# Two-layer diffusion backbone: one turn for the context units' weights, the keys' rotation summed on VectorE, and new planning constants

## The chip, the cores and the metric

The kernel runs on one core of a Trainium2 chip. The metric is the device time of one execution in microseconds (us). The core has five engines that are named here as the profile names them: PE (TensorE, the matmuls), DVE (VectorE), ACT (ScalarE), POOL (GpSimd) and SP (SyncE, which here issues DMAs). PEld is the loading of stationary operands into PE. A `q` behind an engine (SPq, ACTq) marks what its sequencer does, such as issuing a DMA.

## The reference

512 latent tokens and 256 context tokens, all of width 1024, go through two layers. Both layers share this frame:

```python
h = rms_norm(x, pre_g[i]) * (1.0 + scale) + shift
hc = rms_norm(xc, pre_g[i]) * (1.0 + cscale) + cshift
...
x = x + gate * rms_norm(y, post_g[i])
if not last:
    xc = xc + cgate * rms_norm(yc, post_g[i])
```

`shift`, `scale` and `gate` come from a product of a conditioning vector with `ada_w`. The mixer of layer 0 is differential attention with 8 heads of two 64-wide halves, that of layer 1 is attention with 8 query heads of width 128, two key and value heads, and normalised queries and keys. Both rotate the queries and keys of the latent tokens. Context queries see context keys alone, latent queries see all 768 keys. The result of a head is multiplied by `silu(z)`, and `w_out` maps the branch back to 1024 columns.

```python
o1 = sweep_attention(qq[..., 0, :], kk[..., 0, :], vv)
o2 = sweep_attention(qq[..., 1, :], kk[..., 1, :], vv)
o = o1 - lam.astype(o1.dtype) * o2
o = rms_norm(o, subln_g) * (1.0 - lam_init)
return (o.reshape(o.shape[0], o.shape[1], BRANCH_WIDTH) * jax.nn.silu(gate)) @ w_out
```

```python
def apply_rope(x, cos, sin):
    x1, x2 = jnp.split(x, 2, axis=-1)
    return jnp.concatenate([x1 * cs - x2 * sn, x2 * cs + x1 * sn], axis=-1)
```

In layer 1 only the latent tokens have queries, since the context's result is not used.

## The kernel before

**Precision.** Each projection multiplies a high and a low half of both operands: `mm3` (L174 and on) issues three matmuls, high by high, high by low, low by high, through `tmm` (L166 to L172, so L170 stands for most matmuls of the trace). A weight is loaded by SP into `raw`, cast to its high half on ACT (L249, `whi`), and the rest is taken by `pieces` (L240 to L243, `wlo`) on DVE, or on POOL in pieces of 256 columns.

**Layer 0, attention.** `s_units` makes one unit per 128 queries: scores on PE (L1055 for a latent unit, L1087 for a context one), maximum on DVE (L1060), exponential on ACT (L1063), the difference of the two softmaxes on DVE, then `f_split` makes two float16 halves of the weights: `fp` by ACT (L291) and DVE (L1025). `f_turn` (L1030) turns them so that keys stand on the partitions: a transposing DMA from SP (`turn`, L253 and L254) writes them into `ft`. A tile `ft` of 12 rows of 256 serves two units, the even one's 128 queries in the left half of each row and the odd one's in the right. `unit_ctx` (L1080 and on) does both context units of a head together, for heads 0 to 6: their weights are two times 512 columns, and two DMAs turn them, one for each block of 128 queries. Head 7's context goes through two plain units. `pv_f16` (L184 to L187) multiplies the values with the turned weights, six matmuls of 256 columns for two rows of keys: 18 for a chunk of two latent units, 6 for the context chunk.

**Layer boundary.** Layer 0's output projection and residual end in `h1_tr` (L1401 and on): PE transposes the normalised rows (L1406), DVE and ACT scale and shift four tiles of 256 columns into `hf` (the first HFD of each four on DVE, L1412, the rest on ACT, L1414), ACT casts the high half (L1418) and DVE takes the low half (L1419). The list KV orders the keys' and values' projection: `k` a projection, `t` an `h1_tr`, `c` the transposes of one finished block of keys (`k_tr`, L1473 and on). A block of keys is normalised (`head_rstd`, L1459 to L1466; L1487), rotated by `rope_tok` (products ta, L1452, and tb, L1454, on DVE; their sum on POOL, L1457, written to `kr`), and transposed on PE (L1477). KVE tells on which engine the low halves of weights 8 to 11 are taken (1 is POOL). `rope_tok` also serves the queries of layer 1.

**Layer 1, attention.** `s1_units` makes a unit per 128 queries and head (maximum L1590, exponential L1596, float16 halves L291 and L1602), turned by one full DMA each; `pv1_steps` uses two of them per chunk. `q_proj` and `z1_proj` are the projections that fill the time between. At the end `tail1` splits the results (L1681, L1682) and starts the last output projection on the banks of the scores.

**What sets the order.** The program text is emitted by a planner, `flow`. It keeps a clock of PE time. Each `Step` (a score unit, a use of turned weights, a loading of conditioning weights) has a due time `at` and lags behind other steps; while no step is due, `piece()` emits one matmul triple of the filling work (projections in the order of FILL0 or FILL1). In layer 0 a head's share of the clock is `per = ATT + DL0[h] + filling`, where `filling` is 7.7 us for a `z` and 15.4 us for a `qk` or a `v` that HF0 lists for that head; its six units are due at even distances over `per - GAP0 + jt[5]`, jt being the row of JT for that layer and head. `acc_steps` spreads the conditioning weights' steps over the heads by ACCN. In layer 1 a unit is due at

```python
st_.at = at_ + TS * (h * 2 + ch + i / 2) + jt[0][5]
```

where `at_` is AT1 after the first queries' projection. A use of turned weights is due LA + jt[0] after its last unit and LT + jt[1] after the use before it; a score unit waits SLAG (SLAG1 in layer 1) + jt[4] behind an earlier one; LM and jt[2] are lags of a step for the output; HOT0, HOT1 and jt[3] are priorities. The framework then arranges the instructions of each engine by these priorities. Tile names that occur below: `sc` scores in PSUM, `p` exponentials, `vp` values, `gT` and `g1` (shown as `g`) results, `araw` and `gw` conditioning weights, `xn` normalised rows.

Of the kernel before, what the change touches and what calls it, by code (L numbers as in the profile page):

```python
# [12 lines left out]
ALU = mybir.AluOpType  # L13
# [6 lines left out]
P = 128  # L20
# [9 lines left out]
SC_A = 64 ** -0.5  # L30
SC_B = 128 ** -0.5
HOT = 1357
HF0 = ((('z', 0), ('qk', 1), ('qk', 2), ('qk', 3)), (), (('z', 1), ('qk', 4), ('v', 2), ('z', 2)), (), (('qk', 5), ('z', 3), ('v', 4), ('qk', 6), ('z', 4)), (), (('qk', 7), ('z', 6), ('v', 6), ('z', 5), ('z', 7)), ())
FILL0 = tuple(f for hf in HF0 for f in hf)
ATT = 15.11
ACCN = (1, 0, 4, 2, 4, 0, 3, 4)
ACD = 1.77
FILL1 = (('q', 1), ('z', 2), ('z', 0), ('q', 2), ('q', 3), ('z', 1), ('z', 3), ('z', 4), ('z', 6), ('z', 5), ('z', 7))
HOT0 = (3826, 1502, 326, 3469)
HOT1 = (2169, 4095, 3201, 5846, 2552, 918)  # L40
WARM = 3008
AGB = 10
PRE = 19.12
TS = 8.25
HFD = 2
KVE = (1, 0, 0, 0)
KV = (('k', 0), ('t', 1), ('k', 2), ('k', 1), ('t', 0), ('c', 1), ('k', 3), ('c', 0), ('k', 4), ('c', 2), ('c', 3), ('k', 5))
SPL = 7.5
GAP0 = 5.92
DL0 = (4.7, -1.53, 0.38, 0.81, 1.04, 3.67, -0.34, 6.0)  # L50
WBUFS = 3
XE = [2, 2, 2, 2, 3, 3]
NWARM = 16
# [18 lines left out]
HFB = 3  # L72
PRI = (3010, 72, 362, 216, 1000)
GD = (2.08, 2.79)
QLAG = 3.92
QTR = 9.95
EG0 = 'a'
EP0 = 'p'
# [2 lines left out]
EG1 = 'a'  # L81
EGA = "v"
RL = 4.05
LM = (4.63, 10.94)
PB0 = 3
FB0 = 2
EF0 = 'a'
VH = 2.6
VPB = 1
FT0 = 3  # L90
JT = (((-1.05, -0.92, 0.68, 2264, 0.12, 3.56), (0, 0.85, 1.39, -990, 0.72, 0.2), (-2.31, -0.09, 3.54, 1893, 0.76, -2.98), (-0.99, -0.17, -1.19, 0, 0.9, 0.95), (0.7, 0.62, -0.38, -4, 2.54, -1.23), (-0.72, 0.43, 0.01, -269, -0.45, -2.95), (1.4, 0.1, 0.12, -328, 0.12, -0.89), (0.18, -0.06, 1.09, 0, -2.44, -0.17)), ((-3.15, 0.21, -0.44, -128, 2.28, 0.69), (1.27, -0.8, -0.1, 65, -0.08, 1.07), (-2.3, -0.84, -1.14, 69, -0.88, 0), (1.25, 0.04, 0, 721, -0.58, -0.62), (0.58, -0.04, 0.52, 604, 0.04, 0.06), (0.41, -0.95, -2.95, 60, -1.31, -1.14), (0.75, -0.49, -1.4, 1427, 0, -1.44), (0.04, 0.48, -1.17, 217, 1.04, 0.15)))


def f32(ap):
# [8 lines left out]
def tile_backbone(  # L103
# [23 lines left out]
    nc = tc.nc  # L127
# [125 lines left out]
    def turn(dst, src):  # L253
        nc.sync.dma_start(dst, src, transpose=True)  # L254
# [604 lines left out]
    with tc.tile_pool(name="t0", bufs=1) as t0:  # L859
# [32 lines left out]
        qk, pend, qk_t = {}, {}, {}  # L892
# [134 lines left out]
        def ft_tile():  # L1027
            return t0.tile([P, 12, 256], F16, tag="ft", name=nm("ft"), bufs=FT0)

        def f_turn(ft, fp, e):  # L1030
            turn(ft[:, :4 * fp.shape[1], e * P:e * P + P], fp.rearrange("p j a n -> p (j a n)"))

        def s_units(h, qts):
            res = []
# [42 lines left out]
            def unit_ctx():  # L1077
                sc = [sc2(), sc2()]
                qh, ql, kh_, kl_ = qk[h]
                prev = None  # L1080
                for qt in (NQ, NQ + 1):
                    tok = slice(qt * P, (qt + 1) * P)
                    for i, (a, b) in enumerate(((qh, kh_), (qh, kl_), (ql, kh_))):
                        for m in (1, 0):
                            r = slice(m * 64, m * 64 + 64)
                            with onward(prev):
                                prev = nc.tensor.matmul(  # L1087
                                    sc[m][:, qt - NQ, :C], a[r, tok], b[r, S:T], start=i == 0, stop=i == 2)
                l = small(4)
                pts = []  # L1090
                for m in range(2):
                    mx = small(2)
                    nc.vector.tensor_reduce(mx, sc[m][:, :, :C], AX.X, ALU.max, negate=True)
                    pt = t0.tile([P, T], F32, tag=f"p{m}", name=nm("p"), bufs=PB0 if m == 0 else 2)
                    pts.append([pt[:, e * C:(e + 1) * C] for e in range(2)])
                    for e in range(2):
                        nc.scalar.activation(pts[m][e], sc[m][:, e, :C], AF.Exp, bias=mx[:, e:e + 1], accum_out=l[:, 2 * m + e:2 * m + e + 1])
                r, f = small(4), small(4)
                nc.vector.reciprocal(r, l)
                nc.vector.scalar_tensor_tensor(f[:, 0:2], r[:, 2:4], nlam, l[:, 0:2], ALU.mult, ALU.mult)  # L1100
                nc.vector.tensor_scalar(f[:, 2:4], r[:, 0:2], psc[:, 0:1], None, ALU.mult)
                fp = f_tile()
                for e in range(2):
                    nc.vector.scalar_tensor_tensor(pts[0][e], pts[1][e], f[:, e:e + 1], pts[0][e], ALU.mult, ALU.add)  # L1104
                    f_split(fp[:, e], pts[0][e], f[:, 2 + e:3 + e])
                res.append(ft_tile())
                for e in range(2):
                    f_turn(res[0], fp[:, e:e + 1], e)

            if qts[0] == NQ and h < KT - 1:  # L1110
                return res, [Step(unit_ctx, 1.0)]
# [244 lines left out]
    c, n = OUTC[0]  # L1356
# [13 lines left out]
    c, n = OUTC[1]  # L1370
# [63 lines left out]
    with tc.tile_pool(name="t1", bufs=1, side="right") as t1p:  # L1434
# [9 lines left out]
        kl = t1p.tile([P, 2, T], F32R, name="kl")  # L1444
        vp = t1p.tile([P, 2, NT, 256], F16, name="vp")

        def rope_tok(dst, src, t):
            n = 2
            s3 = src.rearrange("p (h d) -> p h d", h=n)
            ta_ = t1p.tile([P, n, P], F32, tag="ta", name=nm("ta"), bufs=2)  # L1450
            tb_ = t1p.tile([P, n, P], F32, tag="tb", name=nm("tb"), bufs=1)
            nc.vector.tensor_tensor(ta_, s3, cosb[:, t, :].unsqueeze(1).to_broadcast([P, n, P]), ALU.mult)  # L1452
            for j in range(2):
                nc.vector.tensor_tensor(  # L1454
                    tb_[:, :, j * 64:j * 64 + 64], s3[:, :, (1 - j) * 64:(1 - j) * 64 + 64],
                    sinb[:, t, j * 64:j * 64 + 64].unsqueeze(1).to_broadcast([P, n, 64]), ALU.mult)
            nc.gpsimd.tensor_tensor(dst.rearrange("p (h d) -> p h d", h=n), ta_, tb_, ALU.add)  # L1457
# [25 lines left out]
        def k_rope(m, o, r):  # L1483
            kn = t1p.tile([P, 256], F32, tag="qt", name=nm("kn"), bufs=9)
            for j in range(2):
                sl = slice(j * P, (j + 1) * P)
                nc.vector.scalar_tensor_tensor(kn[:, sl], o[:, sl], r[:, j:j + 1], gq[:, 1, :], ALU.mult, ALU.mult)  # L1487
            close(o)
            if m < NQ:
                kr = t1p.tile([P, 256], F32, tag="qt", name=nm("kr"), bufs=9)  # L1490
                rope_tok(kr, kn, m)
            else:
                kr = kn
            ktr.append((m, kr))
# [260 lines left out]
        c, n = OUTC1[0]  # L1755
# [9 lines left out]
        c, n = OUTC1[1]  # L1765
# [134 lines left out]
```

## Time and profile before

| what | value |
|---|---|
| time, median of 3 runs | 742.33 us |
| lowest and highest of them | 741.08 and 743.64 us |
| profiled execution, its own time | 742.18 us |
| its span, first to last instruction | 740.1 us |
| granted TensorE clock, mean | 0.997 |
| HBM read, written | 70.56 MB, 2.10 MB |

In the profile, busy times are of instructions that do work; issuing a DMA and waiting are not counted. Matmuls are pipelined and their ends are modelled, so the mean duration of one is longer than the distance between two. A row of the timeline gives the start, the duration of the merged instructions, the engine, the line, the operation, output and inputs with their shapes, and the count; in brackets stands the engine's idle time just before it and what ended it. A row of waits gives, for an engine and line, what it waited for, the sum, the number of times and the longest.

### The profile page before, as it was taken

The numbers are of one execution on the slowest core, as the hardware profiler recorded it, in microseconds if no ns is written. First come the engines' busy times: TensorE is split into PE (matmuls) and PEld (weight loads), VectorE is DVE, ScalarE is ACT, GpSimd is POOL, SyncE is SP. The second block draws the span as 40 slices with busy tenths as digits, with TensorE's granted clock in tenths as the row PEclk, the third lists the DMA queues.
The fourth block names the chain that finished last, engine by engine and source line by source line (L and its number), as shares of the span: only waits on it lengthen the run. The fifth ranks groups of instructions, "written<-read, shape, count | busy, mean of one in ns | idle before, by whom it ended". The sixth has DMA issues, their size and how long they took to land. (4 is left out here: it accounts for less than half of the span.)

```text
span 740.1 us, 12749 instructions
## 1 busy us (share of the span) xinstructions
PE 722.6 (98%) x4668; PEld 615.9 (83%) x4668; DVE 523.0 (71%) x947; ACT 484.0 (65%) x1016; POOL 247.4 (33%) x334
## 2 busy tenths in 40 slices
PE   8999999999999999999999999998999999999996
PEld 6789888878987888889878888877998999887785
DVE  4667566789777777777777815387668889877724
ACT  5547456686676685777877734485548777788622
POOL 0110236553412633445131411554452534143101
PEclk9999999999999999999999999999999999999998
DMA  9935363455757434754565207030436798887503
GB/s 332 391 112 196 110 171 94 113 133 147 173 134 192 107 92 113 195 108 138 134 153 146 58 8 255 30 115 19 141 105 138 150 207 183 207 177 130 123 26 113
DMA packets 142093, 104.93 MB, mean 142 GB/s; under 512 B 112464, under 2 KB 115024, under 8 KB 142032
## 3 DMA queue, kind: packets, MB, share of 16 engines
q1 hardware_dynamic: 138176, 98.32, 51.5%
q10 hardware_dynamic: 3856, 5.81, 2.3%
q8 instruction: 36, 0.59, 0.3%
q14 instruction: 25, 0.20, 0.1%
HBM read 70.56 MB, written 2.10 MB: 98 GB/s over the span
## 5 line engine op out<-in xcount | busy, mean ns | idle before, releaser
L170 PE MATMUL bk<-h,whi 128*128 128x512 f32 (+2 forms) x864 | 228.1, 347 | 0.1
L170 PE MATMUL bk<-whi,h 128*128 128x256 f32 (+1 forms) x928 | 214.6, 319 | 0.0
L170 PEld LDWEIGHTS bk<-whi,h 128*128 128x128 f32 x928 | 155.2, 189 | 16.5 <-issue 3.7
L170 PEld LDWEIGHTS bk<-h,whi 128*128 128x128 f32 x864 | 151.0, 188 | 19.2 <-issue 2.7
L170 PE MATMUL bk<-h,wlo 128*128 128x512 f32 (+2 forms) x432 | 149.0, 346 | 0.0
L170 PE MATMUL bk<-wlo,h 128*128 128x256 f32 (+1 forms) x464 | 146.3, 317 | 0.0
L243 DVE TENSOR_TENSOR wlo<-raw,whi 128x1024 fp32r<-128x1024 f32 (+2 forms) x70 | 83.6, 1197 | 21.9 <-ACT whi L249 21.3
L170 PEld LDWEIGHTS bk<-wlo,h 128*128 128x128 f32 x464 | 87.5, 189 | 5.9
L170 PEld LDWEIGHTS bk<-h,wlo 128*128 128x128 f32 x432 | 81.1, 188 | 8.6 <-issue 1.6
L291 ACT ACTIVATE fp<-p,sm 128x768 f16<-128x768 f32 (+1 forms) x80 | 67.6, 851 | 28.6 <-DVE p L1104 9.5
L243 POOL TENSOR_TENSOR sz<-sz,za 128x192 f32<-128x192 f32 (+1 forms) x48 | 34.8, 748 | 151.0 <-ACT za L223 151.0
L187 PE MATMUL bk<-ft,vp 128*128 128x256 f16 x624 | 78.7, 274 | 4.7 <-DMA ft<-fp 4.5
L249 ACT CAST whi<-raw 128x1024 fp32r<-128x1024 f32 x64 | 67.0, 1047 | 22.2 <-PE bk L170 10.1
L187 PEld LDWEIGHTS <-vp 128*128 128x128 f16 x624 | 57.2, 98 | 23.5 <-issue 9.4
L1063 ACT ACTIVATE p<-sc,sm 128x768 f32<-128x768 f32 (+1 forms) x68 | 59.5, 877 | 21.6 <-DVE sm L1060 20.5
L1060 DVE TENSOR_REDUCE sm<-sc 128x1 f32<-128x768 f32 (+1 forms) x68 | 60.6, 918 | 9.6 <-PE sc L1055 9.4
L1025 DVE SCALAR_TENSOR_TENSOR fp<-p,sm,fp 128x768 f16<-128x768 f32 (+1 forms) x48 | 43.8, 922 | 14.1 <-ACT fp L291 13.8
L1055 PE MATMUL sc<-qk,qk 64*128 64x384 f32 (+1 forms) x396 | 43.6, 351 | 0.5 <-ACT p L1063 0.3
L243 POOL TENSOR_TENSOR qk<-qr,qk 128x256 fp32r<-128x256 f32 x42 | 31.7, 790 | 36.2 <-ACT qk L932 36.2
L170 PE MATMUL sc<-whi,h 128*128 128x512 f32 x128 | 41.9, 395 | 1.0 <-ACT p L1596 1.0
L1055 PEld LDWEIGHTS sc<-qk,qk 64*128 64x128 f32 x396 | 32.8, 184 | 8.3 <-issue 4.1
L243 POOL TENSOR_TENSOR qr<-qr,sw 128x256 f32<-128x256 f32 x28 | 24.3, 888 | 39.3 <-DVE sw L917 39.3
(254 smaller groups left out, 1207.7 us busy)
## 6 DMA issues: line engine op xcount, KB each, us to landing
raw<-in_a_w SPq DMA_DIRECT2D x28, 512.0 KB, 3.4
araw<-in_ada_w SPq DMA_DIRECT2D x12, 1024.0 KB, 5.5
raw<-in_b_w SPq DMA_DIRECT2D x20, 512.0 KB, 3.4
ag<-in_ada SPq DMA_DIRECT2D x16, 512.0 KB, 7.9
raw<-in_w_out SPq DMA_DIRECT2D x16, 512.0 KB, 4.6
sw<-qr ACTq DMA_DIRECT2D x32, 128.0 KB, 2.1
gw<-in_ada_w SPq DMA_DIRECT2D x8, 512.0 KB, 4.1
xnt<-in_xlT SPq DMA_DIRECT2D x4, 512.0 KB, 5.9
```

The costliest lines, as they stand in the source:

```text
L170: i = nc.tensor.matmul(o, a, b, start=start, stop=stop)
L187: nc.tensor.matmul(o, v[:, a, kt + e, c], f[:, 2 * b + e, :], start=first and i == 0, stop=last and i == 5)
L243: eng.tensor_tensor(dst[:, i:i + n], a[:, i:i + n], b[:, i:i + n], op)
L249: nc.scalar.copy(hi, r)
L291: nc.scalar.activation(dst, src, AF.Copy, scale=s_)
L1025: nc.vector.scalar_tensor_tensor(fp[..., 1, :], src, r, fp[..., 0, :], ALU.mult, ALU.subtract)
L1055: prev = nc.tensor.matmul(sc[m][:, j if nk == T else m, :w], a[r, tok], b[r, c], start=i == 0, stop=i == 2)
L1060: nc.vector.tensor_reduce(mx, scv, AX.XY if nk == T else AX.X, ALU.max, negate=True)
L1063: nc.scalar.activation(pv_, scv, AF.Exp, bias=mx, accum_out=l[:, m:m + 1])
```

## The change

Four edits of the code, and new values of constants.

- `unit_ctx` turns the weights of both context units with one DMA into the first 1024 columns of the tile's row, block of 128 queries by block. A small class, `CtxF`, gives `pv_f16` the same view as before: for each key row, two runs of 128 columns.
- `rope_tok` has a new argument: the sum of ta and tb is on DVE when it is set. `k_rope` sets it, the queries do not.
- KVE goes from (1, 0, 0, 0) to zeros: the low half of weight 8 is taken on DVE. HFD goes from 2 to 3: of four scalings in `h1_tr` three are on DVE.
- The planner's constants change for both layers. In HF0, `z` 6 is now ahead of `qk` 7, and `z` 7 is counted to head 7 instead of head 6.

```diff
-HF0 = (..., (), (('qk', 7), ('z', 6), ('v', 6), ('z', 5), ('z', 7)), ())
+HF0 = (..., (), (('z', 6), ('qk', 7), ('v', 6), ('z', 5)), (('z', 7),))
-ACCN = (1, 0, 4, 2, 4, 0, 3, 4)
+ACCN = (1, 0, 4, 4, 1, 1, 3, 4)
-HOT1 = (2169, 4095, 3201, 5846, 2552, 918)
+HOT1 = (2621, 4095, 3201, 5846, 2552, 801)
-TS = 8.25
-HFD = 2
-KVE = (1, 0, 0, 0)
+TS = 8.28
+HFD = 3
+KVE = (0, 0, 0, 0)
-DL0 = (4.7, -1.53, 0.38, 0.81, 1.04, 3.67, -0.34, 6.0)
+DL0 = (4.7, -1.53, 2.15, 0.81, 1.04, 3.37, -0.34, 6.0)
-LA = (12.0, 7.03)
-LT = (1.27, 1.11)
+LA = (12.0, 6.91)
+LT = (1.27, 0.75)
-SLAG1 = 2.79
-AT1 = 7.65
+SLAG1 = 1.91
+AT1 = 6.52
-QLAG = 3.92
+QLAG = 4.06
-LM = (4.63, 10.94)
+LM = (4.63, 10.89)
-JT = (((-1.05, -0.92, 0.68, 2264, 0.12, 3.56), (0, 0.85, 1.39, -990, 0.72, 0.2), (-2.31, -0.09, 3.54, 1893, 0.76, -2.98), (-0.99, -0.17, -1.19, 0, 0.9, 0.95), (0.7, 0.62, -0.38, -4, 2.54, -1.23), (-0.72, 0.43, 0.01, -269, -0.45, -2.95), (1.4, 0.1, 0.12, -328, 0.12, -0.89), (0.18, -0.06, 1.09, 0, -2.44, -0.17)), ((-3.15, 0.21, -0.44, -128, 2.28, 0.69), (1.27, -0.8, -0.1, 65, -0.08, 1.07), (-2.3, -0.84, -1.14, 69, -0.88, 0), (1.25, 0.04, 0, 721, -0.58, -0.62), (0.58, -0.04, 0.52, 604, 0.04, 0.06), (0.41, -0.95, -2.95, 60, -1.31, -1.14), (0.75, -0.49, -1.4, 1427, 0, -1.44), (0.04, 0.48, -1.17, 217, 1.04, 0.15)))
+JT = (((-1.05, -0.92, 0.68, 2264, 0.12, 3.56), (0, 0.85, 1.39, -990, 0.72, 0.2), (-1.79, -0.04, 3.05, 2086, 0.25, -3.11), (-1.27, -0.19, -1.34, -101, 0.52, 1.62), (0.7, 0.62, -0.38, 172, 2.54, -1.23), (-2.89, 0.39, 0.58, -269, -0.21, -5.24), (1.4, 0.1, 0.12, -328, 0.12, -0.89), (0.18, -0.06, 1.09, 0, -2.44, -0.17)), ((-3.15, 0.14, -0.44, 0, 1.76, 0.45), (1.27, -0.86, -1.1, 65, 0.0, 1.07), (-2.3, -0.67, -1.14, -156, -1.53, 0), (1.25, 0.05, 0.3, -218, -0.19, -0.62), (3.23, 0.88, 1.15, 604, -2.1, 0), (0.41, -0.95, -4.08, 60, -1.31, -0.92), (0, -0.65, -0.83, 1758, 0, -2.55), (-0.45, 0.78, -0.94, -466, 1.04, 0.14)))
...
+        class CtxF:
+            def __init__(self, ft):
+                self.f = ft.rearrange("p j n -> p (j n)")[:, :1024].rearrange("p (e j n) -> p j e n", e=2, n=P)
+
+            def __getitem__(self, i):
+                return self.f if i[1] == slice(0, 4) else self.f[:, i[1]]
...
-                res.append(ft_tile())
-                for e in range(2):
-                    f_turn(res[0], fp[:, e:e + 1], e)
+                ft = ft_tile()
+                turn(ft.rearrange("p j (b n) -> p (j b) n", n=P)[:, :8], fp[:, :2].rearrange("p e a n -> p (e a n)"))
+                res.append(CtxF(ft))
...
-            nc.gpsimd.tensor_tensor(dst.rearrange("p (h d) -> p h d", h=n), ta_, tb_, ALU.add)
+            (nc.vector if ev else nc.gpsimd).tensor_tensor(dst.rearrange("p (h d) -> p h d", h=n), ta_, tb_, ALU.add)
...
-                rope_tok(kr, kn, m)
+                rope_tok(kr, kn, m, True)
```

More of the change, by code (lines that the diff above doesn't have):

```diff
@@ L32 @@
 HOT = 1357
-HF0 = ((('z', 0), ('qk', 1), ('qk', 2), ('qk', 3)), (), (('z', 1), ('qk', 4), ('v', 2), ('z', 2)), (), (('qk', 5), ('z', 3), ('v', 4), ('qk', 6), ('z', 4)), (), (('qk', 7), ('z', 6), ('v', 6), ('z', 5), ('z', 7)), ())
+HF0 = ((('z', 0), ('qk', 1), ('qk', 2), ('qk', 3)), (), (('z', 1), ('qk', 4), ('v', 2), ('z', 2)), (), (('qk', 5), ('z', 3), ('v', 4), ('qk', 6), ('z', 4)), (), (('z', 6), ('qk', 7), ('v', 6), ('z', 5)), (('z', 7),))
 FILL0 = tuple(f for hf in HF0 for f in hf)
 ATT = 15.11
-ACCN = (1, 0, 4, 2, 4, 0, 3, 4)
+ACCN = (1, 0, 4, 4, 1, 1, 3, 4)
 ACD = 1.77
@@ L1445, in tile_backbone, with rope_tok @@
         vp = t1p.tile([P, 2, NT, 256], F16, name="vp")
-        def rope_tok(dst, src, t):
+        def rope_tok(dst, src, t, ev=False):
             n = 2
```

## Prediction

> **What bounds the kernel now.** I read the page first, then PE's waits by releaser, then the stages, and last the timeline around each wait. The first lines are the page's, the next are those of PE's waits (total us, times, longest), the last are rows of the stage table (length, PE, PEld, DVE, ACT and POOL busy).
>
> ```profile
> span 740.1 us, 12749 instructions
> ```
>
> ```profile
> PE 722.6 (98%) x4668; PEld 615.9 (83%) x4668; DVE 523.0 (71%) x947; ACT 484.0 (65%) x1016; POOL 247.4 (33%) x334
> ```
>
> ```profile
> PE bk L187 <- DMA ft<-fp: 4.5, 4, 1.8
> PE bk L1477 <- POOL kr L1457: 1.9, 1, 1.9
> PE sc L170 <- ACT p L1596: 1.0, 1, 1.0
> ```
>
> ```profile
> 0.00:45.00 45.00, 41.95 (x306) 31.69 (x307) 28.38 (x83) 24.66 (x50) 4.56 (x11) 1.00 0.90 331
> 234.00:265.00 31.00, 29.41 (x210) 26.18 (x209) 23.85 (x38) 21.71 (x49) 13.58 (x16) 1.00 0.49 112
> 370.00:410.00 40.00, 38.23 (x283) 31.83 (x283) 30.29 (x53) 29.66 (x63) 11.84 (x16) 1.00 0.56 139
> 470.00:532.00 62.00, 59.84 (x315) 49.47 (x314) 43.60 (x85) 38.73 (x111) 30.77 (x52) 1.00 0.23 71
> 532.00:600.00 68.00, 67.86 (x495) 64.66 (x495) 52.66 (x117) 47.52 (x110) 28.19 (x42) 1.00 0.61 141
> 660.00:690.00 30.00, 27.27 (x155) 22.95 (x154) 24.41 (x42) 25.67 (x44) 10.81 (x12) 1.00 0.66 124
> 690.00:741.00 51.00, 44.00 (x213) 35.91 (x211) 22.84 (x35) 15.86 (x34) 4.72 (x12) 0.95 0.33 94
> ```
>
> TensorE is the bound: 722.6 of 740.1 us. No matmul is added or removed, so the change can only act through the 17.5 us in which PE is idle. Of these the first 45 us hold 3.05 and the last stage 6.1 (51.00 less 0.9 beyond the span, less 44.00); both run code that the diff leaves alone. What is left to win is 1.59 + 1.77 + 2.16 + 0.14 + 2.73 = 8.4 us, five stages with a handful of waits. What can be lost has no such limit: PE works through its queue in the order that is set, so any producer that is late by an order set anew stops it.
>
> **The change part by part.**
>
> *The keys' sum on VectorE.* The longest single wait of the layer boundary, row by row (start, duration, engine, line, what it waited for in brackets), and below it the groups that price the sum on either engine:
>
> ```profile
> 512.87 0.42 DVE L1452 TENSOR_TENSOR ta<-kn,ropeb 128x256 f32<-128x256 f32 x1
> 513.21 0.49 DVE L1454 TENSOR_TENSOR tb<-kn,ropeb 128x128 f32<-128x128 f32 x2
> 513.62 0.68 DVE L1419 TENSOR_TENSOR h<-hf,h 128x512 fp32r<-128x512 f32 x1
> 513.78 1.10 POOL L1457 TENSOR_TENSOR kr<-ta,tb 128x256 f32<-128x256 f32 x1 [1.59 <-DVE tb L1454]
> 514.94 0.44 PE L1477 MATMUL bk<-ident,kr 128*128 128x128 f32 x2 [1.94 <-POOL kr L1457]
> ```
>
> ```profile
> L1457 POOL TENSOR_TENSOR kr<-ta,tb 128x256 f32<-128x256 f32 x4 | 3.3, 830 | 5.6 <-DVE tb L1454 5.6
> L1481 DVE TENSOR_TENSOR kl<-bk,kh 128x256 fp32r<-128x256 f32 x5 | 2.1, 414 | 0.0
> ```
>
> On POOL the sum ran 513.78 to 514.88. On VectorE a sum of this shape takes 0.41 us and can follow tb at 513.70: it ends at 514.11 if nothing is put between, 0.77 us sooner, and at 514.8 if one 0.68 us pass of h goes first, 0.1 sooner. The order in the queues is planned too, and a sum that is known to end sooner may have its transposes put elsewhere; then all 1.94 goes. So the gain is 0.1 to 1.94, and I take 1.2, between the row's 0.77 and the whole wait. The four sums add 4 x 0.41 = 1.7 us to VectorE, which is 43.60 us busy of 62 here. Behind each stand the h passes of the boundary, for which the next projection waits.
>
> In the rows above, the POOL sum that starts within the h pass of VectorE took 1.10 us, where its group's mean is 0.83. [...]
>
> *Weight 8's low half on VectorE, three scalings of four on VectorE.* First the one line's instructions in a window, then groups (count, busy us, mean ns):
>
> ```profile
> L243 POOL TENSOR_TENSOR wlo<-raw,whi x4: 737/740/741, 461.2 to 463.3; 128x256 fp32r<-128x256 f32 x4
> ```
>
> ```profile
> L243 DVE TENSOR_TENSOR wlo<-raw,whi 128x1024 fp32r<-128x1024 f32 x6 | 7.7, 1277 | 1.6 <-ACT whi L249 1.5
> L1412 DVE TENSOR_SCALAR hf<-sc,mods 128x256 f32<-128x256 f32 x12 | 6.0, 539 | 0.8 <-PE sc L1406 0.4
> L1414 ACT ACTIVATE hf<-sc,mods 128x256 f32<-128x256 f32 x12 | 6.1, 562 | 4.3 <-DVE hf L1412 4.3
> ```
>
> The view that gives the first row lists nobody as waiting for POOL's four pieces (4 x 0.74 = 3.0 us); one VectorE pass of 1.28 replaces them, off the path. Six of twelve ACT scalings (0.56) become VectorE ones (0.54): +3.2 us on VectorE, -3.4 on ACT. The casts on ACT can start after two of four either way, so the latency of an h tile stays. Both at 0, covered by the projections between; if that cover is gone, a held-up h pass costs its 0.54 at each of six places, 3.2 us. With all of it VectorE is at 43.6 + 1.7 + 1.3 + 3.2 = 49.8 of 62, still under PE.
>
> *One turn for a context unit.* Two 512-column turns become one of 1024, for heads 0 to 6 (head 7 keeps its two units). The fourth unit's rows; the landing times of its two turns; that of the one full turn (1536 columns) issued from 259.5 to 260.5; and the list of DMA issues with the count of all turns and their median landing:
>
> ```profile
> 250.37 1.83 DVE L1025 SCALAR_TENSOR_TENSOR fp<-p,sm,fp 128x256 f16<-128x256 f32 x2
> 251.36 2.50 SPq L254 DMA_TRANSPOSE ft<-fp  x2
> 255.12 0.83 PE L187 MATMUL bk<-ft,vp 128*128 128x256 f16 x6 [1.21 <-DMA ft<-fp]
> ```
>
> ```profile
> DMA to landing us min/median/max: 2.4/2.4/2.4
> ```
>
> ```profile
> DMA to landing us min/median/max: 3.6/3.6/3.6
> ```
>
> ```profile
> ft<-fp SPq DMA_TRANSPOSE x80, 4.0
> ```
>
> Before, one issue takes 2.50 / 2 = 1.25, so the second half goes out at 252.6 and lands at 252.6 + 2.4 = 255.0. The joint turn must wait for the second half of fp (250.37 + 1.83 = 252.2) and, by halves between 2.4 and 3.6, needs about 3.0: 255.2. So where VectorE writes the halves far apart, the joint turn is 0.2 late; where both are ready at once it lands after 3.0, not 1.25 + 2.4 = 3.65: 0.6 sooner. What it surely saves is 7 x 1.25 = 8.8 us of SP's queue. On PE's path: -0.6 to +0.2 per wait, taken into the waits below. [...]
>
> The matmuls now read the turned weights in two runs of 128 columns, 42 of 624. No row shows such a read. At best nothing changes (fewer columns are not read, so no gain); at worst each matmul takes its time twice, by the row of layer 1's end below (18 in 2.14, 0.12 each) 42 x 0.12 = 5.0 us. I take 0, since the number of columns stays and the matmul rows of 256 columns that I quote are all contiguous, so nothing speaks for a price; the far end is counted with the slower case.
>
> *Layer 0's order.* The waits here, and what the queue held:
>
> ```profile
> 377.65 0.37 SPq L868 DMA_DIRECT2D araw<-in_ada_w  x1
> 378.11 0.46 SPq L247 DMA_DIRECT2D raw<-in_w_out  x1
> 378.66 3.64 SPq L254 DMA_TRANSPOSE ft<-fp  x2
> 383.31 1.32 PE L1055 MATMUL sc<-qk,qk 64*128 64x384 f32 x12 [0.31 <-ACT p L1063]
> 385.94 0.81 PE L187 MATMUL bk<-ft,vp 128*128 128x256 f16 x6 [1.32 <-DMA ft<-fp]
> ```
>
> Head 6's context weights wait behind two loads. By the diff z 7 (7.7 us of filling in the plan) goes from head 6's budget to head 7's, so head 6's units are spread over 7.7 us less; its context unit (place 4 of 6) comes 7.7 x 4/6 = 5.1 sooner, less 1.47 by which the DL0 sums of heads 0 to 5 grow: 3.7 us, against a wait of 1.32. Head 7's units start 7.7 - 1.47 = 6.2 sooner and are spread over 7.7 more. I take -1.2 of 0.31 + 1.32 (bounds -1.63, and +1.3 for a like wait elsewhere). For head 3 the plan puts the weights' use 0.28 sooner after each unit (JT -0.99 to -1.27), and two of its three uses wait already (1.21 above, and part of the 0.38 that is left of its stage's 1.59): 2 x 0.28 = 0.56 worse; with the SP queue freer, +0.5. Head 5's use comes 2.17 sooner; whether that has cover no wait row tells, since it waits nowhere now.
>
> *Layer 1's order.* The end of its attention:
>
> ```profile
> 674.54 5.05 SPq L254 DMA_TRANSPOSE ft<-fp  x2
> 681.48 2.14 PE L187 MATMUL bk<-ft,vp 128*128 128x256 f16 x18 [1.77 <-DMA ft<-fp]
> 685.65 0.50 PE L170 MATMUL sc<-whi,h 128*128 128x512 f32 x1 [0.96 <-ACT p L1596]
> ```
>
> PE has run out of filling at 679.7 and stands until head 6's last weights land, then until the last softmax frees its banks. A unit is due at AT1 + TS (2h + ch + i/2) + JT's last figure. For head 6 that is -1.13 + 0.03 x 13 - 1.11 = -1.85 us, for head 7 -1.13 + 0.45 - 0.01 = -0.69. Units that come sooner leave filling for the end: up to 1.77 and 0.69 go, 2.46 in all; I take 2.0 (bounds 0 and 2.73). The first use of layer 1 (0.14 in its stage) moves 0.12 sooner after its unit: +0.1.
>
> *Sum.* -1.2 - 1.2 + 0.5 - 2.0 + 0.1 = -3.8. A plan with all due times changed will also be late somewhere that is on time now: I allow one wait of the mean size seen, 4.5 / 4 = 1.1. That leaves -2.7. The profiled execution took 742.18 us (span 740.1 and 2.1 around it), 0.15 under the median of 742.33: 739.5 against it, **739.6** as a median.
>
> **The rivals.** A measurement tells about 0.3% from no change here, 2.2 us: under 740.1 is faster, over 744.6 slower.
>
> *The waits only move.* All 80 turns go out by one queue, which the loads of weights share; an order that frees one use delays another. For it: the four waits for ft (4.5 us) sit in four places with different causes. Then only the keys' sum is won, against nothing else: 742.3 - 1.2 = 741.1.
>
> *The port.* The two engines hold each other up, as the 1.10 us sum showed, now with VectorE as the one that waits. POOL's passes of this shape (0.83 to 1.10 by the rows of kr) are longer than the 0.41 us sum, and one of 1.10 ahead of it eats the 0.77 gained and 0.33 more; with the ordering gains halved (1.4): 742.3 + 0.3 - 1.4 = 741.2. Against it: POOL is busy 30.77 of that stage's 62 us, and 3.3 of them are the sums that leave. [...]
>
> *Layer 1's uses come before their weights* (slower). LA falls by 0.12, and with JT the use moves sooner by 0.87 for head 6, 0.61 for head 7, 0.12 for heads 0 to 3 and 5: over two chunks each 2 x (0.87 + 0.61 + 5 x 0.12) = 4.2 us, if no chunk has cover: 742.3 - 1.2 + 4.2 = 745.3. It decides once a chunk's weights land less than that before use. Against it: of 16 chunks only two wait now, 0.14 and 1.77, and between 600 and 660 PE never stops (the stage's row; below it the group of all uses):
>
> ```profile
> 600.00:660.00 60.00, 60.00 (x387) 53.39 (x386) 51.60 (x104) 46.20 (x86) 21.28 (x25) 1.00 0.89 191
> ```
>
> ```profile
> L187 PE MATMUL bk<-ft,vp 128*128 128x256 f16 x624 | 78.7, 274 | 4.7 <-DMA ft<-fp 4.5
> ```
>
> **How the numbers follow.** Forecast 0.47 (faster), waits only move 0.31 and the port 0.08 (both within 0.3%), uses before weights 0.14 (slower). From these 0.47, 0.39, 0.14. The range runs from 737.0, near the sum without the allowance and with the kept ends of the keys' sum and layer 1's end (-3.8 - 0.74 - 0.73 = -5.3), to 743.5, which takes in both middle cases with one more wait of 1.8, and leaves out the slower case and little below.
>
> **What would show it.** Right: no wait of PE for kr, or one under 1 us; kr on VectorE at 0.41; seven turns fewer (73 of 80), about 3 us to land for the joint ones; PE idle between 660 and 690 under 1 us and between 370 and 410 under 1; PE busy still 722 to 723. Wrong: PE waits for ft of more than 5.6 us in all, a new wait for h at 490 to 525, or L187's mean above 274 ns.

## The result, and the profile after

| what | before | after |
|---|---|---|
| time, median of 6 runs each | 742.77 us | 738.15 us |
| lowest and highest | 741.08 and 743.64 us | 737.64 and 739.19 us |
| ratio to before, 95% interval | | 0.9939 [0.9928, 0.9950] |
| profiled execution, its own time | 742.18 us | 739.19 us |
| its span | 740.1 us | 737.4 us |

The change takes 4.6 us off. The profiled execution of after is the slowest of its six, and the one with the lowest mean granted clock, 0.995 (the others have 0.998 or 0.999). The page of after (span; busy time of the engines):

```profile
span 737.4 us, 12733 instructions
PE 724.0 (98%) x4668; PEld 617.4 (84%) x4668; DVE 527.5 (72%) x958; ACT 481.8 (65%) x1010; POOL 239.4 (32%) x326
```

PE's waits by releaser (total us, times, longest):

```profile
PE bk L187 <- DMA ft<-fp: 2.2, 3, 1.5
PE bk L469 <- ACT ac L467: 1.9, 1, 1.9
...
PE sc L170 <- ACT p L1603: 0.5, 1, 0.5
```

The stage table (length, then busy us of PE, PEld, DVE, ACT, POOL, the granted clock, DMA share, GB/s):

```profile
0.00:45.00 45.00, 42.62 (x310) 32.53 (x311) 28.29 (x83) 24.96 (x50) 5.52 (x11) 1.00 0.90 331
234.00:265.00 31.00, 31.00 (x224) 27.09 (x223) 23.53 (x36) 24.07 (x52) 12.78 (x16) 1.00 0.45 121
370.00:410.00 40.00, 38.15 (x278) 31.94 (x277) 29.23 (x51) 30.33 (x64) 12.60 (x17) 1.00 0.55 139
470.00:532.00 62.00, 62.00 (x345) 52.58 (x344) 49.32 (x101) 39.02 (x115) 27.23 (x48) 1.00 0.25 82
532.00:600.00 68.00, 67.30 (x487) 63.62 (x486) 53.84 (x113) 47.03 (x104) 26.44 (x39) 1.00 0.65 147
660.00:690.00 30.00, 27.61 (x145) 22.75 (x144) 25.19 (x45) 25.11 (x43) 8.66 (x9) 0.94 0.69 151
```

Length less PE busy is PE's idle time. Beside the rows of before, stage by stage:

| stage | idle before | idle after | step of the prediction |
|---|---|---|---|
| 234 to 265 (head 3) | 1.59 | 0 | +0.5 |
| 370 to 410 (head 6) | 1.77 | 1.85 | -1.2 |
| 470 to 532 (boundary) | 2.16 | 0 | -1.2 |
| 532 to 600 | 0.14 | 0.70 | +0.1 |
| 660 to 690 (end of layer 1) | 2.73 | 2.39 | -2.0 |
| sum | 8.39 | 4.94 | -3.8, with a new wait of 1.1: -2.7 |

The sum moved by -3.45, near the -3.8, but hardly by its terms: the stage that was to get worse lost all its idle time, and of the three that were to win, two kept most of theirs. With -0.67 from the first 45 us, which the diff leaves alone (in ten profiles of this study the same stage held between 2.38 and 4.15 us of idle), and +1.4 of PE busy (724.0 less 722.6), the span's -2.7 is complete. The +1.4 goes, by estimate, with the clock of 0.94 in the last row, where before had 1.00: 0.06 of 30 us is 1.8. The profiled executions differ by 3.0 us, the medians by 4.6; the last section sets the clocks of the executions beside that.

What holds the two stages. The timeline of after around head 6's context weights, SP's queue first, then PE, and how long the joint turn took to land:

```profile
375.41 0.37 SPq L868 DMA_DIRECT2D araw<-in_ada_w  x1
375.90 0.43 SPq L247 DMA_DIRECT2D raw<-in_w_out  x1
376.53 2.79 SPq L254 DMA_TRANSPOSE ft<-fp  x1
```

```profile
381.50 1.32 PE L1062 MATMUL sc<-qk,qk 64*128 64x384 f32 x12 [0.32 <-ACT p L1070]
384.35 0.82 PE L187 MATMUL bk<-ft,vp 128*128 128x256 f16 x6 [1.53 <-DMA ft<-fp]
```

```profile
DMA to landing us min/median/max: 7.8/7.8/7.8
```

The turn goes out 2.1 us sooner than before (376.53 against 378.66), the use comes 1.6 us sooner (384.35 against 385.94), the same two loads are ahead of it in the queue, and it lands 7.8 us after its issue. The wait has moved with its surroundings. In before, behind the same two loads, the two half turns already took 6.7 and 4.8 us to land.

The end of layer 1's attention, ACT, then PE, then rows of the stage table for three stretches of 1 us, in which the granted clock is the third figure from the end:

```profile
676.38 2.68 ACT L1688 CAST h<-g 128x512 fp32r<-128x512 f32 x5
678.97 1.04 ACT L249 CAST whi<-raw 128x1024 fp32r<-128x1024 f32 x1
679.92 0.61 ACT L467 CAST ac<-gate 128x512 fp32r<-128x512 f32 x1
680.44 0.98 ACT L1603 ACTIVATE p<-sc,sm,qrs 128x768 f32<-128x768 f32 x1
```

```profile
680.58 0.50 PE L469 MATMUL bk<-ac,ones_r 128*128 128x512 f32 x1 [1.91 <-ACT ac L467]
681.57 0.50 PE L170 MATMUL sc<-whi,h 128*128 128x512 f32 x1 [0.49 <-ACT p L1603]
```

```profile
682.00:683.00 1.00, 1.00 (x5) 0.81 (x4) 1.00 (x2) 1.00 (x3) 0.33 (x1) 0.74 0.00 0
683.00:684.00 1.00, 1.00 (x4) 0.72 (x4) 0.97 (x5) 0.88 (x3) 0.22 (x1) 0.50 0.00 0
684.00:685.00 1.00, 1.00 (x4) 0.81 (x3) 1.00 (x2) 1.00 (x2) 1.00 (x1) 0.50 0.36 61
```

Head 6's last weights now land in time: the wait for ft of 1.77 is gone. In its place ACT is behind. Five casts of `tail1` (of its splits of heads 0 to 6, line 1681 of before) go first and take 2.68 us; a weight's cast and `ac` come next, and the exponential of the last unit but one after that, at 680.44. PE stands 1.91 us for `ac` and 0.49 for the exponential, and then works at half clock for 3.4 us (682.5 to 685.9; the row of 685 to 686 has 0.55, that of 686 to 688 1.00). ACT's rows of before show the same five casts and the weight's cast ahead of the same exponential, for which PE waited 0.96 there; only `ac` stood behind it:

```profile
680.97 2.69 ACT L1681 CAST h<-g 128x512 fp32r<-128x512 f32 x5
683.56 1.05 ACT L249 CAST whi<-raw 128x1024 fp32r<-128x1024 f32 x1
684.51 0.99 ACT L1596 ACTIVATE p<-sc,sm,qrs 128x768 f32<-128x768 f32 x1
```

### The profile page after: what moved, and what is told of

It is laid out like the page before. It is cut to its first block, busy times and chain, and to the rows that moved or that the text cites. A ratio compares the mean times of both kernels' runs of the same rounds, so it can differ in the third digit from the quotient of the medians.

```text
span 737.4 us, 12733 instructions
## 1 busy us (share of the span) xinstructions
PE 724.0 (98%) x4668; PEld 617.4 (84%) x4668; DVE 527.5 (72%) x958; ACT 481.8 (65%) x1010; POOL 239.4 (32%) x326
## 4 chain that ended last, share of the span: by engine, by line
PE 90%; DMA 6%; DVE 1%; ACT 1%; issue 1%; SPq 0%; DVEq 0%; ACTq 0%
PE bk L170 59%; PE sc L170 12%; PE bk L187 9%; PE sc L1062 5%; DMA ft<-fp 2%; DMA ag<-in_ada 2%; PE bk L878 1%; DMA xnt<-in_xlT 1%; PE sc L1094 1%; PE sc L1413 1%; DMA raw<-in_w_out 1%; PE bk L469 1%; PE bk L470 0%; PE bk L1553 0%; DVE h L1689 0%
## 5 line engine op out<-in xcount | busy, mean ns | idle before, releaser
L187 PE MATMUL bk<-ft,vp 128*128 128x256 f16 x624 | 79.6, 274 | 2.2 <-DMA ft<-fp 2.2
L187 PEld LDWEIGHTS <-vp 128*128 128x128 f16 x624 | 57.1, 98 | 21.5 <-issue 12.9
L1603 ACT ACTIVATE p<-sc,sm,qrs 128x768 f32<-128x768 f32 x32 | 31.6, 988 | 12.2 <-DVE sm L1600 7.7
```

The lines of the kernel that those rows point to most:

```text
L187: nc.tensor.matmul(o, v[:, a, kt + e, c], f[:, 2 * b + e, :], start=first and i == 0, stop=last and i == 5)
L1603: nc.scalar.activation(pt.rearrange("p (j n) -> p j n", j=2), scv, AF.Exp, scale=sr, bias=nmx, accum_out=l)
```

## The experiments

Each time is a median, with its ratio to the kernel before and the 95% interval. Every kernel ran on one chip beside the kernel before (there were three such chips, with medians of before from 742.4 to 743.0), so two experiments are best compared by their ratios. "Under after" means the difference from after's 738.15, ratio 0.9939 [0.9928, 0.9950]. Lines shift by seven between kernels with and without `CtxF`, and by two more where the exponentials are collected in a list.

### One part alone

**The keys' sum on VectorE.**

```diff
-            nc.gpsimd.tensor_tensor(dst.rearrange("p (h d) -> p h d", h=n), ta_, tb_, ALU.add)
+            (nc.vector if ev else nc.gpsimd).tensor_tensor(dst.rearrange("p (h d) -> p h d", h=n), ta_, tb_, ALU.add)
```

> The kernel before with the keys' sum on VectorE and nothing else. Theory (a wait of PE for kr, 1.94 us, is what this part is worth, by itself): no wait of PE for kr is left, 1.2 to 2.0 us faster, ratio 0.9973 to 0.9984. Rival (the gain comes from the orders set anew, the sum alone only moves the wait): a wait of about 1.2 us for kr stays or another takes its place, under 0.8 us faster, ratio above 0.9989.

Measured 741.66 us, 0.9989 [0.9976, 1.0003]: no change that can be told. The place in the timeline:

```profile
514.22 0.50 PE L170 MATMUL bk<-whi,h 128*128 128x512 f32 x1 [1.67 <-DVE kl L1481]
```

The wait for kr is gone and one of 1.67 for kl stands in its place. `kl`, the low half of another key block, is on VectorE behind ta, tb and an h pass, and PE's next projection needs the bank that it reads. The rival held by the trace, and by the time at its edge: VectorE's queue is the next limit here, and a sum that moves to it moves the wait.

**One turn for a context unit.**

```diff
-                res.append(ft_tile())
-                for e in range(2):
-                    f_turn(res[0], fp[:, e:e + 1], e)
+                ft = ft_tile()
+                turn(ft.rearrange("p j (b n) -> p (j b) n", n=P)[:, :8], fp[:, :2].rearrange("p e a n -> p (e a n)"))
+                res.append(CtxF(ft))
```

> The kernel before with the context units' weights turned by one transfer and nothing else. Theory (a joint turn lands no sooner, 3.0 to 7.8 us after its issue, and the SP time saved was idle): within 0.6 us of before, PE's waits for ft stay at 4 to 5 us. Rival (the freed SP queue and the sooner landing remove the context waits of 1.21 and 1.32 us): 1.2 to 2.5 us faster, waits for ft under 3.3 us.

Measured 742.52 us, 0.9999 [0.9985, 1.0013]. Two of its waits (head 3's and head 6's context weights):

```profile
255.52 0.81 PE L187 MATMUL bk<-ft,vp 128*128 128x256 f16 x6 [1.54 <-DMA ft<-fp]
...
386.17 0.81 PE L187 MATMUL bk<-ft,vp 128*128 128x256 f16 x6 [1.08 <-DMA ft<-fp]
```

Against 1.21 and 1.32 the first is 0.33 longer and the second 0.24 shorter: the two cases that the prediction named, a half that came early and two that were ready at once. The theory held. Six matmuls with their weights in two runs still take 0.81 us, so the read costs nothing.

**The boundary's three edits together** (the sum, weight 8's low half, three scalings of four on VectorE).

```diff
-HFD = 2
-KVE = (1, 0, 0, 0)
+HFD = 3
+KVE = (0, 0, 0, 0)
...
-                rope_tok(kr, kn, m)
+                rope_tok(kr, kn, m, True)
```

> The kernel before with the keys' sum, weight 8's low half and three scalings of four on VectorE. Theory (at the boundary PE waits for whatever the chain of one block of keys gives last; taking POOL out moves the wait to VectorE's kl or h): a wait of 1 us or more stays between 505 and 525, 0.5 to 1.2 us faster, ratio 0.9984 to 0.9993. Rival (the three edits together empty the chain): no wait there, 2 to 3.6 us faster, ratio 0.995 to 0.997.

Measured 741.07 us, 0.9978 [0.9967, 0.9989], 1.9 faster. PE's one wait at the boundary:

```profile
492.02 0.73 PE L170 MATMUL bk<-whi,h 128*128 128x512 f32 x2 [0.91 <-DVE h L1419]
```

Neither kr nor kl is waited for; an h pass on VectorE is, 0.91 us, twenty us sooner, where VectorE has the added scalings (that these make the wait was not tried by itself). So the place at 505 to 525 is emptied, at the price of a smaller wait. The theory had a wait of 1 us or more staying there and failed; the rival's place was right, and its 2 to 3.6 us were just missed. The stage's idle time fell by 1.17 (2.16 to 0.99), so the rest of the 1.9 lies elsewhere or is noise; the last section returns to it.

**Layer 0's constants.**

```diff
-HF0 = (..., (), (('qk', 7), ('z', 6), ('v', 6), ('z', 5), ('z', 7)), ())
-ACCN = (1, 0, 4, 2, 4, 0, 3, 4)
-DL0 = (4.7, -1.53, 0.38, 0.81, 1.04, 3.67, -0.34, 6.0)
+HF0 = (..., (), (('z', 6), ('qk', 7), ('v', 6), ('z', 5)), (('z', 7),))
+ACCN = (1, 0, 4, 4, 1, 1, 3, 4)
+DL0 = (4.7, -1.53, 2.15, 0.81, 1.04, 3.37, -0.34, 6.0)
...
```

> The kernel before with HF0, ACCN, DL0 and layer 0's part of JT as after. Theory (these constants removed head 3's two waits, 1.44 us, and left the one at head 6's end): 1.0 to 1.8 us faster, no wait of PE between 234 and 265, 1.5 to 2.2 us idle between 370 and 410. Rival (the parts only work together, since one order is made of all): within 0.6 us of before or slower, waits elsewhere.

Measured 738.26 us, 0.9944 [0.9925, 0.9963]: 4.2 faster, by itself nearly what the whole change gives, and far more than the theory (1.0 to 1.8) or its rival allowed. Its waits and stages:

```profile
PE bk L170 <- DVE kl L1481: 0.7, 1, 0.7
...
PE bk L1477 <- POOL kr L1457: 0.2, 1, 0.2
```

```profile
234.00:265.00 31.00, 31.00 (x224) 27.08 (x223) 23.00 (x35) 24.05 (x52) 12.76 (x16) 1.00 0.45 117
370.00:410.00 40.00, 38.44 (x281) 32.23 (x281) 29.52 (x52) 30.62 (x64) 12.88 (x17) 1.00 0.57 139
470.00:532.00 62.00, 61.09 (x334) 51.18 (x334) 44.01 (x87) 40.01 (x115) 30.57 (x50) 1.00 0.24 79
```

Head 3's waits are gone, head 6's are 1.56 of 1.77, and at the boundary, whose code is that of before with the sum still on POOL, 0.91 is left of 2.16. The theory had the first two stages right and left out the third: the boundary gained from an order that was set two stages ahead of it.

**Layer 1's constants.**

```diff
-TS = 8.25
-LA = (12.0, 7.03)
-SLAG1 = 2.79
-AT1 = 7.65
+TS = 8.28
+LA = (12.0, 6.91)
+SLAG1 = 1.91
+AT1 = 6.52
...
```

> The kernel before with HOT1, TS, LT, LA, SLAG1, AT1, QLAG, LM and layer 1's part of JT as after. Theory (layer 1's constants won nothing: the 2.7 us idle at the end of its attention become 2.4, a drop of the granted clock to 0.5 behind them costs 1.5): 0 to 1.5 us slower than before, the clock at 0.5 for some us after 680. Rival (they are worth the rest of the 4.6 us): 1.5 to 2.7 us faster, no such drop.

Measured 744.34 us, 1.002 [1.0007, 1.0033]: slower by 1.9. A stage that had no idle time has 1.27 now, in one wait:

```profile
600.00:660.00 60.00, 58.73 (x385) 52.55 (x384) 50.99 (x104) 46.45 (x93) 21.29 (x26) 1.00 0.85 189
```

```profile
605.60 2.14 PE L187 MATMUL bk<-ft,vp 128*128 128x256 f16 x18 [1.27 <-DMA ft<-fp]
```

This is the slower rival of the prediction, at one chunk of sixteen. The theory had 0 to 1.5 slower with a drop of the clock behind 680; the clock stays at 1.00 there. This execution does have 3.4 us of half clock, but behind the wait of 1.94 for kr that ends at 514.54; the one of before has a wait of 1.94 for kr too, and 1.00 behind it (last section). That drop is not the whole 1.9: among the executions with a mean granted clock of 0.998 or more the median is 743.4 (7 of 12), against 741.8 for before on that chip (15 of 29).

### Layer 0's constants taken apart

One kernel has only HF0 of them, as in this diff, the next has ACCN, DL0 and the first half of JT and leaves HF0 as it was:

```diff
-HF0 = (..., (), (('qk', 7), ('z', 6), ('v', 6), ('z', 5), ('z', 7)), ())
+HF0 = (..., (), (('z', 6), ('qk', 7), ('v', 6), ('z', 5)), (('z', 7),))
```

> The kernel before, with only HF0 of the change: z 6 ahead of qk 7, z 7 counted to head 7. Theory (it is this order that moves head 6's units and head 7's): half or more of what all of layer 0's constants gave, 740.3 or less, with the wait near 384 us shorter than 1.3. Rival, that the due times of heads 2 to 5 (DL0, ACCN, JT) hold the gain: 742 or more, with the waits of 250 to 256 us unchanged (0.23 and 1.21).

> The kernel before, with layer 0's other constants of the change (ACCN, DL0, the first half of JT) but HF0 as it was. Theory that HF0 holds half or more of the gain: 740.3 or more. Rival, that these due times hold it: 739 or less, with no wait at 250 to 256 us.

HF0 alone: 747.73 us, 1.0067 [1.0053, 1.0081], 4.8 slower. The others alone: 740.98 us, 0.9978 [0.9967, 0.9988], 1.9 faster. Together they gave -4.2. By their bounds the first run speaks for the due times and the second for HF0; what holds is neither alone: HF0 is worth about -2.2 where the due times go with it (-4.2 less -1.95, each against before on its own chip) and +4.8 where they don't. The stage rows of head 3 and of the boundary, first with HF0 alone, then with the others alone:

```profile
234.00:265.00 31.00, 29.58 (x216) 26.14 (x213) 23.86 (x39) 21.70 (x48) 13.68 (x17) 1.00 0.50 119
470.00:532.00 62.00, 62.00 (x305) 50.95 (x304) 42.66 (x79) 37.67 (x106) 29.70 (x51) 1.00 0.18 56
```

```profile
234.00:265.00 31.00, 31.00 (x224) 27.08 (x223) 22.92 (x35) 24.07 (x52) 12.78 (x16) 1.00 0.45 120
470.00:532.00 62.00, 59.84 (x318) 49.60 (x317) 43.99 (x86) 38.73 (x111) 30.87 (x51) 1.00 0.22 71
```

So the two halves act in two places. The due times free head 3 and leave the boundary as it was, with 2.16 idle and the wait of 1.9 for kr. HF0 leaves head 3 waiting, and no wait of PE at the boundary is listed with it (up to 545, since all is later in that kernel). What HF0 alone costs lies between them. The two scores of 256 columns in before, then PE's timeline with HF0 alone and its granted clock:

```profile
408.96 0.62 PE L1055 MATMUL sc<-qk,qk 64*128 64x256 f32 x6
420.62 0.62 PE L1055 MATMUL sc<-qk,qk 64*128 64x256 f32 x6
```

```profile
408.33 0.62 PE L1055 MATMUL sc<-qk,qk 64*128 64x256 f32 x6
413.42 1.01 PE L1055 MATMUL sc<-qk,qk 64*128 64x256 f32 x6 [4.47 <-ACT p L1063]
416.14 4.02 PE L187 MATMUL bk<-ft,vp 128*128 128x256 f16 x18 [1.72 <-DMA ft<-fp]
```

```profile
410.00:415.00 5.00, 1.01 (x6) 0.71 (x6) 3.61 (x9) 2.53 (x7) 4.39 (x6) 0.58 0.29 57
417.00:420.00 3.00, 3.00 (x16) 2.19 (x15) 1.62 (x10) 0.51 (x1) 0.00 (x0) 0.50 0.21 44
```

These are head 7's two context units, the only scores of 256 columns at L1055. In before 11 us of other matmuls stand between them. Here nothing does: PE waits 4.47 for an exponential and then 1.72 for turned weights, and works at half clock from 410.8 to 421.0, by the rows of 0.58 and 0.50 and one of 0.90 from 420 to 425. Filling was left, since projections follow from 419.81 on; the order has put it behind. Why these due times do so with the new HF0 was not traced.

### One part taken back

**The sum back on POOL**, all else as after (`rope_tok(kr, kn, m)`).

> The kernel after with the keys' sum back on POOL. Theory (layer 0's constants alone left only 0.2 us of the wait for kr, so the sum is worth little here): 0 to 1 us slower than after, ratio to before 0.9935 to 0.9955, a wait for kr under 0.5 us. Rival (the sum is what removed the wait, and with it a drop of the granted clock): the wait of 1.9 us is back, 2 to 3.6 us slower than after, ratio 0.9965 to 0.999.

Measured 738.56 us, 0.9942 [0.9923, 0.9961], 0.4 over after, which is within the intervals, as the theory had it. The stage from 470 to 532 has no wait for kr, kl or h in it. With layer 0's new order and the boundary's two other edits in place, the place of the sum does not matter.

**Layer 0's constants back**, all else as after.

> The kernel after, with layer 0's planning constants those of the kernel before (HF0, ACCN, DL0, the first half of JT); everything else of the change stays. By the single parts (joint turn 0, boundary -1.9, layer 1 +1.9) it takes about 742.5, as the kernel before, and the waits for turned weights at 250 to 256 and at 384 us are back. Rival, that the gain comes from the parts together and layer 0's order is only the part that lets it be seen: 740 or less.

Measured 741.44 us, 0.9984 [0.9976, 0.9993]. It lies between the theory and its rival, 1.1 under the sum of the single parts. Head 3's stage is at 29.28 us busy of 31 again, and at the boundary the wait of 0.9 for h is there as in the kernel with the boundary's edits alone. Layer 1's constants cost 1.9 alone and about 0.4 beside the boundary's edits (741.44 less 741.07, within the intervals), which is what the sum missed.

**Layer 1's constants back**, all else as after.

> The kernel after with layer 1's constants as before. Theory (those constants cost by themselves, 1.9 us when they were set alone): 1 to 2 us faster than after, ratio 0.991 to 0.993, no wait for ac at the end of layer 1's attention. Rival (the parts only fit together): same as after or slower, ratio over 0.9935.

Measured 736.79 us, 0.9924 [0.9905, 0.9942]: 1.4 under after, as expected, and no wait for `ac`. The interval overlaps that of after, so this run by itself is a sign only; with the +1.9 of these constants alone it says that they win nothing, and probably cost time inside the change too.

### The end of layer 1

With after as it is, the casts of heads 2 to 6 are held behind the exponential of the last unit but one:

```diff
+        exps = []
...
-                nc.scalar.activation(pt.rearrange("p (j n) -> p j n", j=2), scv, AF.Exp, scale=sr, bias=nmx, accum_out=l)
+                exps.append(nc.scalar.activation(pt.rearrange("p (j n) -> p j n", j=2), scv, AF.Exp, scale=sr, bias=nmx, accum_out=l))
...
-            split_g1(range(KT - 1))
+            split_g1(range(2))
+            with tc.issue_after(exps[-2].ins):
+                split_g1(range(2, KT - 1))
```

> The kernel after, with the casts of heads 2 to 6 for the last output projection held behind the exponential of the last unit but one. Theory (PE's 2.4 us at the end of layer 1's attention wait for that exponential, which stands on ACT behind five casts and a weight's; the idle time in turn lets the granted clock fall to 0.5 for 3.4 us in some executions): idle there under 0.8 us, no drop, 1.2 to 2.4 us faster than after, ratio 0.9905 to 0.9925. Rival (the low halves on VectorE, 0.83 us each, are then late for PE): idle of 1 us or more stays in several pieces, within 0.6 us of after.

Measured 736.62 us, 0.9920 [0.9901, 0.9939], 1.5 under after, again with overlapping intervals. What the trace shows is clearer. PE's idle time between 660 and 690 falls from 2.39 to 0.74, as the theory had it, and the wait for `ac` from 1.9 to 0.3:

```profile
PE bk L469 <- ACT ac L467: 0.3, 1, 0.3
```

So the casts on ACT made that wait. Both cures together:

> The kernel after, with two edits together: layer 1's planning constants those of the kernel before, and at the end of layer 1's attention the casts of heads 2 to 6 held behind the exponential of the last unit but one. Each alone took about 1.4 us from the kernel after (736.79 and 736.62). Theory that the two act on different waits (the constants on the turned weights' waits between 600 and 690 us, the casts on the wait for the last exponential): about 735.2, with no wait for ac and at most 0.5 for p at the end. Rival, that both cures remove the same thing, the one gap near 680 us and the drop of the granted clock behind it: 736.6, no better than one alone.

Measured 735.91 us, 0.9912 [0.9897, 0.9926], the lowest of the study: 2.2 under after, with intervals that just do not overlap. It lies between the theory and its rival, and the 0.7 under one cure alone is within the intervals, so the time does not tell whether the two cures add. On ACT the exponential is now ahead of three of the five casts and of `ac`, 2.2 us sooner than in after (678.20 against 680.44), and PE waits neither for `ac` nor for that exponential:

```profile
677.25 1.05 ACT L249 CAST whi<-raw 128x1024 fp32r<-128x1024 f32 x1
678.20 0.99 ACT L1605 ACTIVATE p<-sc,sm,qrs 128x768 f32<-128x768 f32 x1
...
679.18 1.65 ACT L1690 CAST h<-g 128x512 fp32r<-128x512 f32 x3
```

What is left there is a wait of 1.34 for head 6's weights before 676.76. That wait belongs to layer 1's old constants (1.49 with these alone put back): with the casts held and the new constants, 0.74 was left in this stage.

## Why the prediction was right in its direction and partly wrong in its reasons

Right:

- PE is the bound, and only its idle time could move. Its instructions stay 4668, and the gain is idle time of the named stages (-3.45).
- The joint turn is worth about 0 (measured 0.9999 [0.9985, 1.0013]), late where the halves come apart and early where they come together. There are 73 turns, and the read in two runs costs nothing (L187's mean stays 274 ns).
- The sum takes 0.41 to 0.42 us on VectorE in three of four cases. The fourth took 0.84, while POOL worked on the rotation's table (L1524, two in 1.67 us from 515.34). That would fit the rival "the port"; what held the sum up was not shown, and nobody waited for it. Of the four sums on POOL in before three took 0.73 to 0.74 and one 1.10; VectorE was at work during a part or all of each.
- There is one new wait, allowed at 1.1; `ac` has 1.9.

Of the signs that the prediction named, four did not come: PE's idle time under 1 us at head 6 (1.85) and at layer 1's end (2.39), PE busy at 722 to 723 (724.0), and about 3 us for a joint turn to land at head 6 (7.8; head 3's took 3.1 in the kernel with the joint turn alone).

Wrong, by step:

- **The keys' sum, -1.2.** The wait went, but not by this edit: alone it leaves 1.67 for kl, and taken back it costs 0.4, within the intervals. The step priced the one chain that the row showed, ta, tb, sum, transposes, and not the VectorE queue that all the boundary's chains share. Freed of the wait for one key block, PE stops at the next item of that queue. "The waits only move" was right at this place, which it left out.
- **Layer 0's order, -1.2 for head 6.** Measured +0.08. The working put the unit 3.7 us sooner against an unmoved use. The turn went out 2.1 sooner, of which 1.6 is head 3's idle time that went, so in its surroundings it moved by 0.5, and the use came 1.6 sooner as well. The turn landed 7.8 us after its issue, not the 3.0 that I took from turns with nothing ahead of them; at this place the two halves had taken 6.7 and 4.8 in before. Two loads are still ahead of it.
- **Head 3, +0.5.** Measured -1.59, a wrong sign. I read one constant of its row (jt[1], 0.28 sooner) and left the others (spread over 1.62 less 0.95 = 0.67 us more, more steps of conditioning weights by ACCN, head 2's longer share). The run without HF0 (31.00 busy of 31) shows that these due times do it.
- **Layer 1's end, -2.0.** Measured -0.34. The mechanism came about: the weights landed in time and the 1.77 went. But ACT's queue, which no term of mine held, was the next in line. The working gave 0.69 of the wait of 0.96 to head 7's due time and called its exponential the last; it is that of the last unit but one, and in before too it started only when the five casts and a weight's cast ahead of it were done (680.97 to 684.5). Units that are due sooner do not move it past them. ACT's rows of before for 680 to 685 should have been listed.
- **What was not there at all**: that layer 0's order reaches the boundary (2.16 to 0.91 with no edit there, by HF0), and that PE's clock fell behind some of its waits (to 0.5 for 3.4 us in after's profile, 1.7 us of PE's work by estimate).

So that the time came out within 1.5 us was in good part luck: the sum's terms were off by up to 2.1 us each, in both directions. The single parts give -4.2 (layer 0), -1.9 (boundary), 0 (turn), +1.9 (layer 1), -4.2 in all against the -4.6 measured; but HF0's two prices and layer 1's 0.4 to 1.9 show that they don't simply add.

Open: which of ACCN, DL0 and JT's rows frees head 3 and carries HF0, and by what chain HF0 shortens the wait at the boundary. These were not tried one by one.

## What to carry to other kernels

A wait that the profile shows ended, in these runs, when its releaser's engine got round to it (1.67 us for kl, 1.91 for `ac`): before pricing a faster step, list what else that engine owes to the bound engine in the next two or three us, since the second in line is the new wait. An order of work and the due times that are fitted to it are one edit; half of it can cost more than the whole gains (+4.8 us for HF0 alone, -4.2 for layer 0's constants together). And when weights at last come in time, look at the next engine of the chain, here ACT, whose queue held work that nobody needed yet ahead of the exponential that PE waited for. The same queue could be read in the trace of before.

## What the runs showed of the hardware

No term of mine held a price for the granted clock. In five profiled executions it was 0.5 for some us in or behind waits of PE. Rows of the stage table of merge_alone for three stretches of 2 us, behind a wait of 1.9 for kr, and then those of before for the same stretches, behind the wait of 1.94 for kr (the granted clock is the third figure from the end, and the count behind PE's busy time is that of its matmuls):

```profile
514.00:516.00 2.00, 0.97 (x4) 0.87 (x5) 1.92 (x4) 1.91 (x10) 1.83 (x3) 0.76 0.00 0
516.00:518.00 2.00, 2.00 (x6) 1.60 (x5) 1.61 (x6) 0.13 (x1) 1.24 (x3) 0.50 0.45 96
518.00:520.00 2.00, 2.00 (x9) 1.59 (x8) 1.97 (x8) 0.00 (x0) 1.10 (x2) 0.89 1.03 399
```

```profile
514.00:516.00 2.00, 1.06 (x6) 0.93 (x7) 1.83 (x4) 1.85 (x9) 1.83 (x3) 1.00 0.00 0
516.00:518.00 2.00, 2.00 (x11) 1.64 (x10) 1.69 (x6) 0.00 (x0) 1.16 (x3) 1.00 0.61 93
518.00:520.00 2.00, 2.00 (x10) 1.66 (x9) 1.97 (x7) 0.00 (x0) 1.19 (x2) 1.00 1.04 402
```

From 516 to 518 PE does 6 matmuls at 0.50 and 11 at 1.00. Eight cases, with the time at half clock worked out from such rows:

| execution | PE's waits or idle time | granted clock in or behind them |
|---|---|---|
| after | 1.91 for `ac`, 0.49 for p, to 681.57 | 0.5 for 3.4 us |
| merge_alone | 1.9 for kr | 0.5 for 3.4 us |
| layer1_alone | 1.94 for kr, to 514.54 | 0.5 for 3.4 us (0.71, 0.50, 0.94 in the three stretches) |
| after_pool_sum | 0.84 idle in 380 to 384, 1.28 in 384 to 386 | 0.5 for 3.4 us (0.86, 0.50, 0.78 from 384 in steps of 2 us) |
| layer0_order_only | 4.47 for p, 1.72 for ft, to 416.14 | 0.5 for 10.2 us (410.8 to 421.0) |
| before | 1.94 for kr, to 514.94 | 1.00 |
| before | 1.77 for ft, to 681.48, and 0.96 for p, to 685.65 | 1.00 |
| kr_alone | 1.67 for kl, to 514.22 | 1.00 |

So the length of a wait alone does not tell the clock behind it: 1.94 for kr has 1.00 behind it in before and 0.50 in layer1_alone. What decides was not shown. Where the clock was 0.5 for 3.4 us, half of that, 1.7 us of PE's work, is my estimate of the price. The times agree with it. Before ran 69 times beside the experiments: the 19 executions with a mean granted clock of 0.996 or less have a median of 743.5, the 34 with 0.998 or more one of 741.8, 1.7 less. (The other 16 have 0.997 and times from 741.15 to 743.78; a mean does not tell where the clock fell.) Of after's six, the slowest, 739.19, is the one at 0.995; the others have 0.998 or 0.999 and end at 738.45.

This also bears on what a few results say. Part of the 4.6 us may be clock: 19 of before's 69 executions are at 0.996 or less, and one of after's six. The sum alone on VectorE, with 1.67 in place of 1.94, gains 0.8 in the median, but its 11 executions (of 12) at 0.998 or more have 741.7, as before's 741.8: by this reading it won in the clock alone. The boundary's three edits leave none of their 12 executions at 0.996 or less, against 7 of 17 of before on that chip, which would be the part of their 1.9 that the idle time does not hold. No run was made that changes the clock alone.
